# Two MLP products by halves, with seven partial products for eight, weight sums made by accumulating DMAs, and a token-major second product

## The chip, the cores and the metric

The kernel runs on one core of one Trainium2 chip. Times are microseconds of device time; a matmul means one instruction of TensorE. The kernel moves its data between DRAM and the core's on-chip memory (SBUF) by DMA, and TensorE writes its sums into PSUM, of which eight banks are in use.

## What is computed

One layer of a hybrid decoder on 512 tokens of width 2048: a norm, three token mixers, gates, a merge, an output projection with a residual, then a norm and an MLP with a residual, then a last norm. The change concerns the end of it, all in float32:

```python
x = x + merged @ w_out[l]
h = rmsnorm(x, norm_mlp[l])
x = x + jnp.square(jax.nn.relu(h @ mlp_w1[l])) @ mlp_w2[l]
return rmsnorm(x, final_norm)
```

`mlp_w1` is 2048 x 8192 and `mlp_w2` 8192 x 2048. With 512 tokens these two products are the largest of the layer.

## The kernel before

**Exact halves.** TensorE gets no plain float32. Each operand is split into a high part (a cast to `float32r`, ScalarE, `hl` L810 and `wtiles` L731) and a low part (operand minus high part, VectorE, `sub` L32). A product of two tiles is then three matmuls that add into the same bank: high x high, high x low, low x high (L748 to L750).

**Weights.** `wtiles` loads a slab of 128 x 1024 (512 KB) by a DMA on SP's queue into `wraw` (three buffers), and splits it into `whi` and `wlo` (three buffers each). In the answers of the trace these are `wrw`, `whw` and `wlw` for both MLP products. `gemm` (from L736) takes a slab's eight weight tiles as the stationary operand and 512 tokens as the moving operand: 24 matmuls a slab.

**The MLP.** Features lie on the partitions and tokens run along the row. After the output projection (16 products `wo`), each `x1[j]` is at once scaled by `norm_mlp` and split into `hh` and `ho`, beside the next product. The 1/rms factor R is not in these operands; it is multiplied in later, at the hidden layer. Eight rounds c follow. Each makes 8 hidden tiles `w1_f` (16 slab tiles deep, two slabs each), applies relu, R and a square on ScalarE and VectorE, splits the result into `ah` and `al`, and then runs 16 products `w2_c_j` of 8 tiles each, whose sums VectorE adds to `x1[j]` (L29). In the last round the products 8 to 15 run in two halves of 256 tokens, so that the final norm of the first half lies beside the second. The output leaves feature-major and is transposed on the host.

**What sets the order.** TensorE's order is the program's. On the other engines a list scheduler places instructions at build time, by priority and by its own estimate of when their inputs come; each engine then executes its list strictly in that order and waits where an input is missing. `high_priority` puts the weight path in front. SP's queue issues all DMAs of the kernel.

**Memory.** `acts` holds 32 tiles of the split activations, `stage` three work tiles, `mlp` the residual and part of the split operands. PSUM has two banks for `gps` tiles and six for `ps` tiles.

## Time and profile before

| | us |
|---|---|
| median of three runs | 3062.14 |
| lowest and highest run | 3059.55, 3068.38 |
| span of the profiled execution | 3059.8 |
| TensorE busy in it | 3001.3 |
| VectorE, ScalarE, GpSimd busy | 1557.3, 989.0, 336.8 |
| each of the three groups of matmuls of the first MLP product (`w`<-`hh`, `ho`; about 1024 each), busy | 398 to 399 |

The profiled execution has no other time than its span; it lies within the three runs. A matmul's own duration is longer than the distance to the next one, since matmuls overlap; for time on TensorE the distance between two starts is what counts. The MLP takes the span from about 1650 us to the end.

### The profile page before, as it was taken

To read this page: it belongs to the slowest core of one execution; us is meant where nothing else is said; L and a number is where in the kernel's file an instruction comes from. 1 tells how busy PE (TensorE), PEld (TensorE's weight loads), DVE (VectorE), ACT (ScalarE), POOL (GpSimd) and SP (SyncE) were. 2 spreads that over 40 slices of the span, in tenths; PEclk is the share of its full clock that TensorE was granted. 3 is DMA by queue.
4 is the path that set the end of the run, shared out by engine and by line. 5 is a ranking of instruction groups with operands and counts; after the bars stand their busy time and mean duration, and the time that the engine had idled before them with its cause. 6 is when DMAs were issued, how large, how long until landed. Compare 5 with 4: busy or idle time off the path is not lost.

```text
span 3059.8 us, 36455 instructions
## 1 busy us (share of the span) xinstructions
PE 3001.3 (98%) x14143; PEld 2468.2 (81%) x14143; DVE 1557.3 (51%) x2350; ACT 989.0 (32%) x1224; POOL 336.8 (11%) x572
## 2 busy tenths in 40 slices
PE   8999988999999999999999999999999999999997
PEld 7888776788877777888888888888888888888887
DVE  7766888855664555555334334333333434333335
ACT  6554121234662233422223222122222212222235
POOL 1001766530000000011110000000000000000003
PEclk9999988999999999999999999999999999999999
DMA  5345333445337163655432333333233323323334
GB/s 181 124 162 185 114 103 98 136 131 166 102 103 190 55 186 97 229 165 170 157 98 94 97 99 96 99 98 97 97 97 97 97 96 97 97 96 97 97 97 151
DMA packets 172638, 370.72 MB, mean 121 GB/s; under 512 B 63377, under 2 KB 74385, under 8 KB 171665
## 3 DMA queue, kind: packets, MB, share of 16 engines
q1 hardware_dynamic: 172464, 368.38, 38.2%
q8 instruction: 112, 1.84, 0.3%
q14 instruction: 62, 0.50, 0.1%
HBM read 318.81 MB, written 44.58 MB: 119 GB/s over the span
## 4 chain that ended last, share of the span: by engine, by line
PE 85%; DVE 6%; POOL 3%; DMA 3%; SPq 1%; issue 1%; ACT 0%; DVEq 0%; ACTq 0%; POOLq 0%
PE w L748 15%; PE w L749 15%; PE w L750 15%; PE gt L748 5%; PE gt L750 5%; PE gt L749 5%; PE z L748 2%; PE z L750 2%; PE z L749 2%; PE wo L750 2%; PE up L748 2%; PE wo L748 2%; PE up L750 2%; PE up L749 2%; PE wo L749 2%
## 5 line engine op out<-in xcount | busy, mean ns | idle before, releaser
L731 ACT CAST whw<-wrw 128x1024 fp32r<-128x1024 f32 x264 | 278.0, 1053 | 885.8 <-PE w L749 872.4
L32 DVE TENSOR_TENSOR wlw<-wrw,whw 128x1024 fp32r<-128x1024 f32 x264 | 324.1, 1227 | 405.2 <-ACT whw L731 405.2
L748 PE MATMUL w<-ah,whw 128*128 128x512 f32 (+1 forms) x1088 | 409.9, 377 | 0.1
L750 PE MATMUL w<-ah,wlw 128*128 128x512 f32 (+1 forms) x1088 | 409.7, 377 | 0.0
L749 PE MATMUL w<-al,whw 128*128 128x512 f32 (+1 forms) x1088 | 409.7, 377 | 0.0
L748 PE MATMUL w<-hh,whw 128*128 128x512 f32 x1024 | 398.7, 389 | 0.0
L750 PE MATMUL w<-hh,wlw 128*128 128x512 f32 x1024 | 398.4, 389 | 0.0
L749 PE MATMUL w<-ho,whw 128*128 128x512 f32 x1024 | 398.4, 389 | 0.0
L748 PE MATMUL gt<-uh,whgt 128*128 128x512 f32 x768 | 310.6, 404 | 2.8 <-DVE gz L26 2.8
L750 PE MATMUL gt<-uh,wlgt 128*128 128x512 f32 x768 | 300.6, 391 | 2.0 <-DVE wlgt L32 2.0
L749 PE MATMUL gt<-ul,whgt 128*128 128x512 f32 x768 | 300.2, 391 | 0.0
L29 DVE TENSOR_TENSOR x<-x,w 128x512 f32<-128x512 f32 (+1 forms) x136 | 89.2, 656 | 388.0 <-PE w L750 388.0
L748 PE MATMUL z<-uh,whin 128*128 128x512 f32 x608 | 243.7, 401 | 11.8 <-DVE zs L26 11.8
L750 PE MATMUL z<-uh,wlin 128*128 128x512 f32 x608 | 241.0, 396 | 8.1 <-DVE wlin L32 8.1
L749 PE MATMUL z<-ul,whin 128*128 128x512 f32 x608 | 240.0, 395 | 0.0
L748 PEld LDWEIGHTS w<-ah,whw 128*128 128x128 f32 x1088 | 204.7, 188 | 37.7 <-issue 0.2
L749 PEld LDWEIGHTS w<-al,whw 128*128 128x128 f32 x1088 | 204.7, 188 | 37.5
L750 PEld LDWEIGHTS w<-ah,wlw 128*128 128x128 f32 x1088 | 204.7, 188 | 37.4
L748 PEld LDWEIGHTS w<-hh,whw 128*128 128x128 f32 x1024 | 192.2, 188 | 40.2 <-issue 0.2
L749 PEld LDWEIGHTS w<-ho,whw 128*128 128x128 f32 x1024 | 192.2, 188 | 40.1 <-issue 0.2
L750 PEld LDWEIGHTS w<-hh,wlw 128*128 128x128 f32 x1024 | 192.2, 188 | 39.9
L29 POOL TENSOR_TENSOR acc<-acc,sq 128x512 f32<-128x512 f32 x29 | 49.7, 1713 | 1521.7 <-ACT sq L830 1490.7
(442 smaller groups left out, 4577.8 us busy)
## 6 DMA issues: line engine op xcount, KB each, us to landing
wrw<-in_w SPq DMA_DIRECT2D x264, 512.0 KB, 3.6
wrgt<-in_w_in SPq DMA_DIRECT2D x96, 512.0 KB, 4.0
wrin<-in_w_in SPq DMA_DIRECT2D x76, 512.0 KB, 3.6
wrup<-in_w_up SPq DMA_DIRECT2D x32, 512.0 KB, 4.0
wrwo<-in_w_out SPq DMA_DIRECT2D x32, 512.0 KB, 3.6
gd<-gz SPq DMA_DIRECT2D x48, 256.0 KB, 2.2
gl<-gd SPq DMA_DIRECT2D x48, 256.0 KB, 3.1
zd<-zs SPq DMA_DIRECT2D x21, 256.0 KB, 2.0
```

The lines of the kernel that those rows point to most:

```text
L29: (eng or self.nc.vector).tensor_tensor(out, a, b, ALU.add)
L32: (eng or self.nc.vector).tensor_tensor(out, a, b, ALU.subtract)
L731: nc.scalar.copy(hi, raw)
L748: nc.tensor.matmul(ps, hi[:, ws], xh, start=first, stop=False)
L749: nc.tensor.matmul(ps, hi[:, ws], xl, start=False, stop=False)
L750: nc.tensor.matmul(ps, lo[:, ws], xh, start=False, stop=last)
```

## The change

Both products are made by halves. A product of two matrices, each cut into four quadrants, takes eight products of quadrants; here it takes seven, of sums of quadrants, and the results are combined by additions (the scheme of Strassen and Winograd). The partial products are numbered 1 to 7. Their operands are, for the weights W: 1 is W11, 5 is W11+W12, 6 is W11+W12+W22, 4 is W11+W12+W22+W21, 3 is W22, 7 is W22+W12, 2 is W21. They run in the order 1, 5, 6, 3, 7, 2, 4.

**Weight sums.** `wsums` holds tile A for 1, 5, 6 and 4, tile B for 3 and 7, and tile C for 2. Three quadrants are loaded plainly on SP's queue. The other four are added onto what A or B holds, in place, by DMAs with `accum_op=ALU.add`, which GpSimd issues. After each load or addition the tile is split into `whi` and `wlo`, which still have three buffers each; A has four, B and C share the three of `wraw`.

**First product.** The tokens are halved (256) and the features are halved. After the output projection, `hsums` forms four sums of two scaled tiles on VectorE and splits all seven operands into `hch` and `hcl` (1792 columns). Three of eight tiles are made during the output projection; five lie in memory that the output projection still uses. The unscaled `x1` is transposed by TensorE (16 groups of four), copied by ScalarE and stored to DRAM as `x1d`, token-major. Then 32 units u follow, each of seven products of 24 matmuls with a moving operand of 256 columns, in three banks `ha`, `hc`, `hb`. Banks are used on: product 6 adds onto product 1 in `ha` after ScalarE has copied it to `pk1`, and so on. VectorE combines the results in `hy`, applies relu and the square, and the 512 KB go to DRAM as `hid`. 1/rms squared is applied only after the second product, by `R2`, one value a token.

**Second product.** It is token-major: the activations are the stationary operand, the weights the moving one, 512 columns. Each round c reads four `hid` tiles back; GpSimd forms their sums in `aG`, ScalarE and VectorE split them into `ah` and `al` (six buffers each). For each half n of the output, two weight chains (`ph` 0 and 1, called a and b) run beside each other: a product is 24 matmuls, 12 with a's weights and 12 with b's. For n = 0 the first two products of a stand ahead of those of b. VectorE adds each bank, scaled by `R2`, to the residual `xT`. The last norm works on rows of tokens, and the output needs no transposition.

```diff
+    ORDER = (1, 5, 6, 3, 7, 2, 4)
+    PLACE = {1: 0, 4: 1, 2: 2, 5: 3, 6: 4, 7: 5, 3: 6}
+    BANK = {1: "a", 6: "a", 7: "a", 4: "a", 5: "c", 3: "c", 2: "b"}
+    def sums(self, G, hi, lo, eng=None):
+        a21, a11, a22, a12, s1, s2, s3, s4 = (G[:, q] for q in range(8))
+        self.sub(s1, a21, a22, eng)
+        self.sub(s2, s1, a11, eng)
+        self.sub(s3, a11, a21, eng)
+        self.add(s4, s2, a12, eng)
+        self.hl(G[:, 1:].rearrange("p q t -> p (q t)"), hi, lo)
+    def wsums(self, name, B, pool, order=None):
+        nc = self.nc
+        at = {}
+        def load(c, q):
+            p = pool if c == "A" else None
+            at[c] = (p or self.wp).tile([P, 1024], F32, name=f"w{c}{name}", tag="wA" if p else "wraw", bufs=self.wA if p else self.wraw)
+            nc.sync.dma_start(at[c], B[q])
+            return at[c]
+        def acc(c, q):
+            nc.gpsimd.dma_start(at[c], B[q], accum_op=ALU.add)
+            return at[c]
+        how = {1: lambda: load("A", "11"), 5: lambda: acc("A", "12"), 6: lambda: acc("A", "22"),
+               4: lambda: acc("A", "21"), 3: lambda: load("B", "22"), 7: lambda: acc("B", "12"),
+               2: lambda: load("C", "21")}
+        for i in order or self.ORDER:
+            with self.tc.high_priority(self.wprio):
+                x = how[i]()
+                hi = self.wp.tile([P, 1024], F32R, name=f"wh{name}_{i}", tag="whi", bufs=self.whl)
+                lo = self.wp.tile([P, 1024], F32R, name=f"wl{name}_{i}", tag="wlo", bufs=self.whl)
+                nc.scalar.copy(hi, x)
+                self.sub(lo, x, hi)
+            yield i, hi, lo
+    def w1_mm(self, ps, i, w, hc, ks):
+        for k in ks:
+            ws = slice(k * P, k * P + P)
+            g = slice(256 * self.PLACE[i], 256 * self.PLACE[i] + 256)
+            for q, (a, b) in enumerate(((0, 0), (0, 1), (1, 0))):
+                self.nc.tensor.matmul(ps, w[a][:, ws], hc[k][b][:, g], start=i in (1, 5, 2) and k == 0 and q == 0,
+                                      stop=k == 7 and q == 2, skip_group_check=True)
+    def w1_out(self, u, i, bank, keep, pool, hid):
+        nc = self.nc
+        with self.tc.high_priority(2 * self.wprio):
+            if i in (1, 5, 6):
+                keep[i] = pool.tile([P, 256], F32, name=f"pk{i}_{u}", tag=f"pk{i}", bufs=2)
+                nc.scalar.copy(keep[i], bank[self.BANK[i]])
+            if i == 1:
+                keep["y"] = pool.tile([P, 4, 256], F32, name=f"hy{u}", tag="hy", bufs=2)
+            y = keep["y"]
+            if i == 7:
+                self.sub(y[:, 2], keep[5], bank["a"])
+            elif i == 2:
+                self.add(y[:, 1], bank["b"], keep[1])
+            elif i == 3:
+                self.sub(y[:, 3], bank["c"], keep[6])
+            elif i == 4:
+                nc.scalar.copy(y[:, 0], bank["a"])
+                f = y.rearrange("p q t -> p (q t)")
+                self.stt(f, f, 0.0, f, ALU.max, ALU.mult)
+                nc.sync.dma_start(hid, f)
...
-                        nc.scalar.activation(hi, x1[j], AF.Copy, scale=col("norm_mlp", j))
-                        self.stt(lo, x1[j], col("norm_mlp", j), hi, ALU.mult, ALU.subtract)
+                    if j in (8, 9, 10):
+                        hsums(j - 8)
+                trunk.close()
+                for k in range(3, 8):
+                    hsums(k)
...
+                    for u in range(1, 32):
+                        bank, keep = banks(u), {}
+                        for i, *w in self.wsums(f"u{u}", w1_quadrants(u), mp):
+                            self.w1_mm(bank[self.BANK[i]], i, w, hc, range(8))
+                            self.w1_out(u, i, bank, keep, mp, hid[u])
...
+                    def hidden(u):
+                        with tc.high_priority(2 * self.wprio):
+                            G = mp.tile([P, 8, 256], F32, name=f"aG{u}", tag="aG", bufs=2)
+                            nc.sync.dma_start(G[:, 0:4].rearrange("p q t -> p (q t)"), hid[u])
+                            r = [mp.tile([P, 1792], F32R, name=f"a{q}{u}", tag=f"a{q}", bufs=6) for q in "hl"]
+                            self.sums(G, *r, nc.gpsimd)
+                        return r
+                    def mm2(ps, i, w, aa, ph, t):
+                        for p in range(2):
+                            x = aa[2 * ph + p]
+                            g = slice(256 * self.PLACE[i] + P * t, 256 * self.PLACE[i] + P * t + P)
+                            ws = slice(T * p, T * p + T)
+                            for q, (a, b) in enumerate(((0, 0), (1, 0), (0, 1))):
+                                nc.tensor.matmul(ps, x[a][:, g], w[b][:, ws], start=i in (1, 5, 2) and ph + p + q == 0,
+                                                 stop=ph + p + q == 4, skip_group_check=True)
...
+                            for (i, *w), (_, *w1) in zip(*gens):
+                                for t in range(2):
+                                    ps = bank[self.BANK[i]][t]
+                                    mm2(ps, i, w, aa, 0, t)
+                                    mm2(ps, i, w1, aa, 1, t)
+                                    out2(i, n, ps, t)
```

The scheduler places the rest. On ScalarE, in the middle of the first product, before: casts of slabs (`whw1_f`) and, for each hidden tile, a relu and a cast.

```order
L731 CAST whw1_21_0_15937<-wrw1_21_0_15935 128x1024
L1156 ACTIVATE a19_15857<-w1_19_15796 128x512
L810 CAST ah19_15861<-a19_15857 128x512
L731 CAST whw1_21_8_15967<-wrw1_21_8_15965 128x1024
L731 CAST whw1_22_0_16006<-wrw1_22_0_16004 128x1024
L1156 ACTIVATE a20_15926<-w1_20_15865 128x512
L810 CAST ah20_15930<-a20_15926 128x512
```

The same engine now, unit 17: `whu17_i` is the high part of operand i, `pk1`, `pk5` and `pk6` are copies of banks after products 1, 5 and 6.

```order
L806 CAST whu17_1_17441<-wAu17_17439 128x1024
L836 COPY hy16_17249<-ha16_17214 128x256
L806 CAST whu17_5_17473<-wAu17_17439 128x1024
L825 COPY pk1_17_17469<-ha17_17436 128x256
L825 COPY pk5_17_17501<-hc17_17437 128x256
L806 CAST whu17_6_17504<-wAu17_17439 128x1024
L806 CAST whu17_3_17536<-wBu17_17534 128x1024
L825 COPY pk6_17_17532<-ha17_17436 128x256
L806 CAST whu17_7_17566<-wBu17_17534 128x1024
L806 CAST whu17_2_17597<-wCu17_17595 128x1024
L806 CAST whu17_4_17627<-wAu17_17439 128x1024
```

Before, the casts stood ahead of the work on finished hidden tiles; now the cast of operand 6 stands behind the copy of the bank of product 5. It stands so in 30 of the units 1 to 31.

VectorE at the same place, before: the slabs' subtractions between the work on the hidden tiles.

```order
L32 TENSOR_TENSOR wlw1_21_0_15938<-wrw1_21_0_15935,whw1_21_0_15937 128x1024
L26 TENSOR_TENSOR a19_15857<-a19_15857,R_81 128x512
L26 TENSOR_TENSOR a19_15857<-a19_15857 128x512
L32 TENSOR_TENSOR al19_15862<-a19_15857,ah19_15861 128x512
L32 TENSOR_TENSOR wlw1_21_8_15968<-wrw1_21_8_15965,whw1_21_8_15967 128x1024
```

VectorE now, unit 17: `wlu17_i` is the low part of operand i, `hy17` the combination of the unit's results.

```order
L33 TENSOR_TENSOR wlu17_5_17474<-wAu17_17439,whu17_5_17473 128x1024
L33 TENSOR_TENSOR wlu17_6_17505<-wAu17_17439,whu17_6_17504 128x1024
L33 TENSOR_TENSOR wlu17_3_17537<-wBu17_17534,whu17_3_17536 128x1024
L33 TENSOR_TENSOR hy17_17471<-hc17_17437,pk6_17_17532 128x256
L33 TENSOR_TENSOR wlu17_7_17567<-wBu17_17534,whu17_7_17566 128x1024
L33 TENSOR_TENSOR wlu17_2_17598<-wCu17_17595,whu17_2_17597 128x1024
L33 TENSOR_TENSOR wlu17_4_17628<-wAu17_17439,whu17_4_17627 128x1024
```

In 21 of the units 1 to 31 the subtraction for operand 7 stands behind the combination that reads product 3's bank, as here. On GpSimd, where the first product had nothing but sums of squares, four accumulating DMAs a unit now stand in the order 5, 6, 4, 7, each behind the splits that read its tile.

ScalarE in the second product, at the beginning of round c = 1 (`whv100` are a's weights for n = 0, `whv101` b's, `ah6` and `ah7` the round's third and fourth activation tiles, `ah8` and `ah9` the next round's first):

```order
L806 CAST whv100_1_21400<-wAv100_21398 128x1024
L887 CAST ah6_21116<-aG6_21114 128x1792
L887 CAST ah7_21126<-aG7_21124 128x1792
L806 CAST whv100_5_21417<-wAv100_21398 128x1024
L806 CAST whv101_1_21435<-wAv101_21433 128x1024
L887 CAST ah8_21664<-aG8_21662 128x1792
L806 CAST whv101_5_21454<-wAv101_21433 128x1024
L806 CAST whv100_6_21473<-wAv100_21398 128x1024
L887 CAST ah9_21674<-aG9_21672 128x1792
L806 CAST whv101_6_21478<-wAv101_21433 128x1024
```

Before, ScalarE had only the casts of weights in the second product, apart from the last round; now the casts of activations stand between them.

## Rows read from the trace of the kernel before

**Rows 1.** The page, busy us by engine, and the granted clock in 40 slices.

```profile
PE 3001.3 (98%) x14143; PEld 2468.2 (81%) x14143; DVE 1557.3 (51%) x2350; ACT 989.0 (32%) x1224; POOL 336.8 (11%) x572
PEclk9999988999999999999999999999999999999999
```

**Rows 2.** Stages: us, busy time of each engine, clock, DMA share, GB/s.

```profile
core 0: us, PE busy (x) PEld busy (x) DVE busy (x) ACT busy (x) POOL busy (x), PEclk, DMA share, GB/s
1600.00:1700.00 100.00, 100.00 (x441) 82.44 (x440) 40.49 (x44) 33.01 (x40) 8.74 (x5) 1.00 0.29 97
1700.00:2000.00 300.00, 300.00 (x1325) 248.42 (x1324) 112.90 (x123) 71.33 (x79) 0.00 (x0) 1.00 0.31 98
```

**Rows 3.** Timeline of TensorE, 512 columns: start, duration, instruction; 36 steps apart.

```profile
2984.21 0.39 PE L748 MATMUL w<-ah,whw 128*128 128x512 f32 x1
...
2992.37 0.39 PE L748 MATMUL w<-ah,whw 128*128 128x512 f32 x1
```

**Rows 4.** The same timeline, 256 columns; 48 steps apart.

```profile
3009.80 0.28 PE L748 MATMUL w<-ah,whw 128*128 128x256 f32 x1
...
3015.57 0.28 PE L748 MATMUL w<-ah,whw 128*128 128x256 f32 x1
```

**Rows 5.** Waits of SP's queue: who waited, for whom, us, times, longest.

```profile
SPq L728 <- DVE wlw L32: 1271.6, 253, 9.1
```

**Rows 6.** Groups by line and shape: busy us, mean ns, idle before.

```profile
L731 ACT CAST whw<-wrw 128x1024 fp32r<-128x1024 f32 x264 | 278.0, 1053 | 885.8 <-PE w L749 872.4 <-PE wo L749 8.8 <-issue 4.6
L32 DVE TENSOR_TENSOR wlw<-wrw,whw 128x1024 fp32r<-128x1024 f32 x264 | 324.1, 1227 | 405.2 <-ACT whw L731 405.2
L285 ACT COPY s5es<-s5e 128x256 f32<-128x256 f32 x12 | 4.5, 373 | 15.4 <-PE s5e L276 15.4
L29 DVE TENSOR_TENSOR x<-x,w 128x256 f32<-128x256 f32 x16 | 6.7, 418 | 5.2 <-PE w L750 5.2
L260 ACT COPY s5ET<-s5ETp 128x512 f32<-128x512 f32 x12 | 7.0, 584 | 20.1 <-PE s5ETp L259 20.0
L1137 ACT ACTIVATE hh<-x,pcol 128x512 fp32r<-128x512 f32 x16 | 11.3, 718 | 0.0
L26 POOL TENSOR_TENSOR x<-x,rt 128x256 f32<-128x256 f32 x20 | 19.6, 1017 | 33.6 <-DVE rt L42 33.6
```

**Rows 7.** DMA issues: KB each, median us from issue to landing.

```profile
wrw<-in_w SPq DMA_DIRECT2D x264, 512.0 KB, 3.6
dBKT<-BKT SPq DMA_DIRECT2D x5, 512.0 KB, 2.9
BKTl<-dBKT SPq DMA_DIRECT2D x5, 512.0 KB, 6.8
```

**Rows 8.** Stages at the end, columns as in rows 2.

```profile
3042.00:3044.00 2.00, 1.60 (x12) 1.19 (x10) 0.70 (x2) 0.46 (x2) 2.00 (x3) 1.00 0.51 181
3044.00:3046.00 2.00, 0.70 (x2) 0.30 (x2) 0.42 (x1) 1.25 (x4) 0.94 (x2) 1.00 0.42 153
3046.00:3060.00 14.00, 0.00 (x0) 0.00 (x0) 7.49 (x15) 1.45 (x2) 3.55 (x4) 0.59 0.49 165
```

**Rows 9.** A wait of TensorE in the timeline, and the stages behind it.

```profile
328.19 1.12 PE L259 MATMUL s5ETp<-cst,s5E 128*128 128x128 f32 x4 [3.07 <-POOL s5E L32]
326.00:328.00 2.00, 0.00 (x0) 0.00 (x0) 2.00 (x3) 0.00 (x0) 1.92 (x2) 1.00 0.19 76
328.00:330.00 2.00, 1.81 (x8) 1.29 (x9) 2.00 (x7) 0.59 (x1) 0.14 (x1) 0.55 0.02 4
330.00:332.00 2.00, 2.00 (x9) 1.27 (x8) 2.00 (x7) 0.57 (x1) 0.00 (x0) 0.60 0.10 39
332.00:334.00 2.00, 2.00 (x11) 1.62 (x10) 1.97 (x7) 1.05 (x1) 0.22 (x1) 1.00 0.61 223
```

More of the change, by code (lines that the diff above doesn't have):

```diff
@@ L1 @@
+import contextlib
 import math
@@ new lines, in banks @@
+                def banks(u):
+                    return {q: self.ps(f"h{q}{u}")[:, 0:256] for q in "acb"}
+                gen = self.wsums("u0", w1_quadrants(0), None, (1, 5, 2, 6, 3, 7, 4))
+                bank, keep = banks(0), {}
+                three = [next(gen) for _ in range(3)]
+                for i, *w in three:
+                    self.w1_mm(bank[self.BANK[i]], i, w, hc, range(3))
+                for jb in (0, 2, 1, 3):
+                    for t in range(4):
+                        pt = self.gps(f"xt{jb}{t}")
+                        for q in range(4):
+                            nc.tensor.transpose(pt[:, q * P:q * P + P], x1[4 * jb + q][:, t * P:t * P + P], self.ident)
+                        st = fp.tile([P, T], F32, name=f"xs{jb}{t}", tag="xs", bufs=2)
+                        nc.scalar.copy(st, pt)
+                        nc.sync.dma_start(x1d[t][:, T * jb:T * jb + T], st)
@@ new lines, in main @@
+                pm = self.gps("pms")
+                for t in range(4):
+                    nc.tensor.matmul(pm[:, 2 * t:2 * t + 2], acc[:, t * P:t * P + P], self.onesD[:, 0:2], start=True, stop=True)
+                self.ts(R2, pm[:, 0:8:2], 1e-6, ALU.add)
+                nc.vector.reciprocal(R2, R2)
+                front.close()
+                with mixpool("w1", "right") as mp:
+                    for i, *w in three:
+                        self.w1_mm(bank[self.BANK[i]], i, w, hc, range(3, 8))
+                        self.w1_out(0, i, bank, keep, mp, hid[0])
+                    for i, *w in gen:
+                        self.w1_mm(bank[self.BANK[i]], i, w, hc, range(8))
+                        self.w1_out(0, i, bank, keep, mp, hid[0])
+                    for u in range(1, 32):
+                        bank, keep = banks(u), {}
+                        for i, *w in self.wsums(f"u{u}", w1_quadrants(u), mp):
+                            self.w1_mm(bank[self.BANK[i]], i, w, hc, range(8))
+                            self.w1_out(u, i, bank, keep, mp, hid[u])
@@ L1269, in pack @@
     r["w1"] = slabs(i["mlp_w1"][0], 16)
[L1270 removed]
+    w2 = i["mlp_w2"][0].reshape(8, 2, 2, 2, 128, 2, 2, 512)
+    r["w2"] = np.ascontiguousarray(w2.transpose(0, 6, 1, 3, 5, 4, 2, 7)).reshape(8, 2, 2, 2, 2, 128, 1024)
+    r["final_row"] = np.ascontiguousarray(np.broadcast_to(i["final_norm"][None], (128, 2048)))
     r["glu"] = slabs(i["s5_glu_w"][0], 6)
```

198 lines of the change are left out of this document (104 added, 94 removed).

## Prediction

> **What bounds the kernel now.** I read the page's busy shares first: TensorE is busy 3001.3 of 3059.8 us and its clock row shows full speed nearly everywhere [rows 1]. The table by stages says the same of the MLP: TensorE 300 of 300 us, VectorE 112.90, ScalarE 71.33, the DMA engines at a share of 0.31 for 98 GB/s [rows 2]. Even the hand-over from the output projection to the MLP, between 1600 and 1700, holds no gap [rows 2]. So time in the MLP is matmuls times their step. The timeline of TensorE gives the steps: 36 matmuls of 512 columns in 8.16 us, 0.2267 each [rows 3], and 48 of 256 columns in 5.77 us, 0.1202 each [rows 4]: half the columns cost 53% of the step. The weights are never late: every load of a w slab waits first for the subtraction that frees its buffer, 253 waits, 1271.6 us [rows 5].
>
> **TensorE's own work.** First product, before: 64 x 16 x 3 = 3072 matmuls of 512 columns, 696.4 us, or 21.76 for each of what are now 32 units. After: a unit is 7 products x 8 slabs x 3 matmuls of 256 columns, 168 x 0.1202 = 20.19 us; in all 5376 and 646.2. Second product, before: 2880 of 512 and 384 of 256 columns, 652.9 + 46.2 = 699.1 us. After: 16 passes x 7 x 24 = 2688 of 512, 609.4 us. If TensorE never waits, the gain is 50.2 + 89.7 = 140 us. Seven for eight is 12.5%, but the narrow moving operand takes nearly half of that back in the first product.
>
> **The first product's weights.** Before, each slab had its own load, far ahead. Now four of a unit's seven operands come by adding in place onto the operand before: 1, 5, 6 and 4 in one tile A, 3 and 7 in B. An accumulating DMA may start only when the cast and the subtraction have read the tile, and the next cast only when it has landed. There are three high and three low buffers, so the split of a product cannot begin before TensorE has finished the product three places earlier; the operand of product 1 is therefore split only at the end of the previous unit's 7. From there runs one chain: split 1, add, split 5, add, split 6, subtraction of 3, add (into B), split 7, and the rest of product 7's matmuls, which free the buffer again. A split is a cast of 1.053 and a subtraction of 1.227, 2.28 us [rows 6]; the third matmul needs the low part, so 22 of 24 matmuls, 2.64 us, follow it. With L for one accumulation and 0.4 us for eight hand-overs, the period is 4 x 2.28 + 1.23 + 2.64 + 0.4 + 3L = 13.4 + 3L us. TensorE's 20.19 us hide this only up to L = 2.3.
>
> L has no row. Below: it is a 512 KB load and more, so at least the plain load's 3.6 us [rows 7]; less is excluded. Above: a 512 KB store (2.9) and a load in company (6.8), 9.7 [rows 7]. It is nearest to the plain load plus one more pass of 512 KB, since it reads the old tile as well. At 98 GB/s for a share of 0.31 the engines pass 316 GB/s, so a pass is 1.7 us, and L = 5.3. The add into B (operand 7) is issued 1.23 us behind the fourth add into A (operand 4) on GpSimd's queue and shares the engines with it; I put half of a two-pass transfer, 1.7 us, on it. The period is 13.4 + 15.9 + 1.7 = 31.0 us against 21.76: **+296 us over 32 units.** Each further us of L costs 96.
>
> The Trainium skill bears on L. "DMA: Bandwidth & Descriptors" (Anatomy of one DMA) fits about 2.0 us + bytes/436e3 for a DMA that GpSimd issues, and "Collectives: The Full Stack" (why ReduceScatter is half of AllGather) says that an add needs two source reads. By these an estimate is 2.0 + 2 x 1.2 = 4.4 us, a period of 28.3 and +209, and some 3300 us in all; no run here shows it yet.
>
> **The queues' order** sets a floor under this, whatever L is. In 30 of the 31 later units ScalarE's cast of operand 6 stands behind the copy of product 5's bank, which waits for TensorE. So after product 5 come the drain (0.16), a copy (0.373), a cast and a subtraction, less two matmuls: 2.6 us in which TensorE does nothing. Behind the waiting cast stand casts 3 and 7. In 21 units VectorE's subtraction for 7 stands behind the combination of product 3's bank (0.418) [rows 6]: 1.6 us. Floor: 20.19 + 2.6 + 1.1 = 23.9 us, +68 us over the stage. At L = 5.3 the chain is longer and hides it.
>
> The bank copies (four of 0.373 us a unit), the combinations and the 512 KB store of `hid` lie beside other work: VectorE needs some 11.5 us of a unit, ScalarE 9. The three plain loads of a unit are issued a unit ahead on SP; nothing there is late.
>
> **The second product's weights.** The same three buffers serve two chains, a and b. A pair of half products is 24 matmuls, 5.44 us. Chain b may split 1 when the pair before is at three quarters, and must have 6 ready 6 + 2 matmuls into its pair: 1.36 + 10.88 + 1.81 = 14.05 us for 3 x 2.28 + 2L = 17.4, short by 3.4; operand 7 of b is short by 2 x 2.28 + L - 8.61 = 1.3. So 4.7 us in a pass with n = 1. In a pass with n = 0 the first four half products come singly, and the splits of two activation tiles (1792 columns, by scaling 1.84 and 2.15 us) stand among them on ScalarE and VectorE. Following the same rule I get 2.2 for operand 5 of a, 3.4 and 3.6 for 5 and 6 of b, 1.4 for 7: 10.6. Eight times 15.3 is 122 us against the 89.7 won: **+33 us.** With L = 3.6 the waits are some 7 us per two passes, and the stage is 32 us faster; each us of L costs 50 to 56.
>
> **The hand-overs.** Before they cost nothing [rows 2]. Into the first product: tiles 3 to 7 of `hc` lie in memory that the output projection reads to its end. Per tile two scaled copies (1.44), four sums (1.7), a cast (1.84) and a subtraction (2.15) run in turn through one `hG`, 7.1 us; the 16 copies of the transposes (0.584 each [rows 6]) fit between. Four of these and 4.0 for the first, less 3.2 us of early matmuls: **+29 us** (20 to 40). Into the second: `aG` lies in `hc`'s memory, so the load (3.6), six GpSimd sums at 1.02 [rows 6], a cast and a subtraction come after the last matmul; the third and fourth tile wait for `aG` to come free. The fourth is ready at about 27.5 us, with 5.4 us of matmuls before it: **+22 us** (12 to 35). The end stays: today 15 us from the last matmul to the end [rows 8]; after, the scaling of the last tiles, four table loads and a store give about the same.
>
> **Sum.** 296 + 33 + 29 + 22 = +380 on the profiled span of 3059.8, which is 2.3 below the median of the runs: 3440 in it, 3442 in runs. I say 3440.
>
> **Rivals.** *Short accumulation.* If L is 3.6 to 4.3 the chain is 24.2 to 26.3, hardly over the floor: +78 to +145; the second product -32 to +10; hand-overs +45: 3150 to 3270. For it: the load's 3.6 already holds all fixed time. Against: a second pass and an issue by GpSimd, neither of which the plain load has.
>
> *The DMA engines become the bound.* In a pass of the second product 6 loads and 8 adds of two passes are 11.5 MB; at 316 GB/s that is 36.5 us against 38.1 of TensorE. If an add takes a third pass, it is 50 us, the second product takes 800 us, and in the first L grows past 7.3, period 37 and more: 3670 to 3850. For it: the tightness. Against: 316 GB/s is no proven limit.
>
> *A falling clock.* One wait of 3.07 us of TensorE was followed by 0.55 and 0.60 of granted clock, near 1.2 GHz, for about 4 us [rows 9]. Here product 6 waits 3 to 4 us in each unit. Product 6 at half rate is 2.9 us later, but 7 waits for its add anyway; I count at most 1.2 us a unit, 38 us, inside the range.
>
> *Faster after all: everything is hidden.* With L under 2.3 the period falls below 20.19; if besides the copies and casts of the floor overlap, the stages give 140 back and the hand-overs cost 45 to 51: 2970. It decides at L = 2.3. Against it stand the plain load's 3.6 [rows 7] and the queues' order; with the order alone the same L gives 3060 to 3110.
>
> **How the numbers follow.** Forecast (L from 4.3 to 7, 3270 to 3670): 0.61. Short accumulation: 0.18. Engines as the bound: 0.16. Hidden and faster: 0.03. Hidden but held by the order to no change: 0.02. The range leaves out the slow end of the bound's case and the hidden ones: 3180 to 3720. Measurement tells apart about 0.3%. Faster 0.03, same 0.02, slower 0.95.
>
> **What would show it.** In the profile after: matmuls of the first product at a step near 0.12 us but with idle time of TensorE before products 5, 6 and 7, released by ScalarE's casts and those by DMA; the time from issue to landing of the adds near 5.3 us; 32 equal periods near 31 us. Periods near 24 say the order alone binds; near 20 that all is hidden and I am wrong. The second product should take 720 to 750 us with waits at operands 5 and 6 of b. A DMA share near 1 would speak for the engines, a granted clock under 0.9 over the first product for the third rival. Wrong most easily: L, which has no row, and whether the add into B is late behind the one into A.

## The result

The changed kernel takes 3652.43 us (median; 3064.17 for the kernel before), a ratio of 1.1905 with an interval of 1.1882 to 1.1928: a fifth slower. One of the four runs took 3768.1 us at a granted clock of 0.80 (0.92 to 0.93 in the others); it is left out of the ratio, but not of the median. The forecast was 3440, with a range of 3180 to 3720. The sign, the mechanism and the main price were as forecast; the loss is half as large again (+588 us for +380).

The page of the changed kernel, busy us by engine and the granted clock in 40 slices; before, TensorE was at 98% [rows 1]:

```profile
span 3650.7 us, 41666 instructions
PE 3138.7 (86%) x15933; PEld 2612.1 (72%) x15933; DVE 1897.2 (52%) x2607; ACT 1202.9 (33%) x1451; POOL 658.7 (18%) x929
PEclk9999989999999999997888888888887999999998
```

Its issues of DMAs (KB each, and the median time from issue to landing):

```profile
wAu<-in_w POOLq DMA_DIRECT2D x96, 512.0 KB, 5.5
wAv<-in_w POOLq DMA_DIRECT2D x96, 512.0 KB, 5.5
...
wCu<-in_w SPq DMA_DIRECT2D x32, 512.0 KB, 4.0
wBu<-in_w POOLq DMA_DIRECT2D x32, 512.0 KB, 7.0
```

`wAu`, `wBu`, `wCu` are the tiles A, B, C of the first product, `wAv` those of the second. L, the number without a row, is there now: an addition of 512 KB lands 5.5 us after its issue in A and 7.0 in B; 5.3 and 5.3 + 1.7 were put in. The Trainium skill's "DMA: Bandwidth & Descriptors" (Anatomy of one DMA), with two reads for an addition, gave an estimate of 4.4; the trace says 5.5, and the trace decides.

Two stages of the changed kernel (us, busy time of the engines, clock, DMA share, GB/s): the first product with its head, and the second with its hand-over and the end.

```profile
core 0: us, PE busy (x) PEld busy (x) DVE busy (x) ACT busy (x) POOL busy (x), PEclk, DMA share, GB/s
1651.00:2770.00 1119.00, 831.35 (x5453) 787.00 (x5451) 360.13 (x374) 289.43 (x380) 111.44 (x128) 0.84 0.53 124
2770.00:3651.00 881.00, 701.97 (x2690) 520.33 (x2688) 529.66 (x510) 306.05 (x305) 242.60 (x256) 0.92 0.70 162
```

The MLP's first matmul stands at 1645.7 us before and at 1651.8 now; these 6 us arise ahead of the output projection, where the instructions are the same, and the forecast has no term for them. The first product was forecast at 696 + 296 + 29 = 1021 us and took 1119; the rest at 699 + 33 + 22 and 17 from the last matmul to the end, 771, and took 881. So both stages are about 100 us over. Two groups give the periods: the last operation on a unit's hidden values (32 of them) and the scaled addition of product 2's banks (two a pass, 16 passes); min, median and max in ns, then the first and the last start.

```profile
L43 DVE SCALAR_TENSOR_TENSOR hy<-hy x32: 1218/1226/1226, 1712.7 to 2770.6; 128x1024 f32<-128x1024 f32 x32
L43 DVE SCALAR_TENSOR_TENSOR xT<-ob,R,xT x32: 744/748/753, 2849.5 to 3612.3; 128x512 f32<-128x512 f32 x32
```

A unit takes (2770.6 - 1712.7) / 31 = 34.13 us; 31.0 was forecast. A pass takes (3612.3 - 2849.5 - 3.4) / 15 = 50.6 us by this group (3.4 is the distance of a pass's two). That is too little: the last pass runs product 2 two places earlier, so that its distance is 33.9 us; the other 14 average 51.8. Below, a pass is counted from its first matmul to the next pass's, as the mean of rounds 1 to 6: 57.0 us for n = 0 and 47.1 for n = 1, where 38.1 + 10.6 = 48.7 and 38.1 + 4.7 = 42.8 were forecast.

### The profile page after: what moved, and what is told of

The parts are those of the page before. It is cut to its first block, busy times and chain, and to the rows that moved or that the text cites. A ratio compares the mean times of both kernels' runs of the same rounds, so it can differ in the third digit from the quotient of the medians.

```text
span 3650.7 us, 41666 instructions
## 1 busy us (share of the span) xinstructions
PE 3138.7 (86%) x15933; PEld 2612.1 (72%) x15933; DVE 1897.2 (52%) x2607; ACT 1202.9 (33%) x1451; POOL 658.7 (18%) x929
## 5 line engine op out<-in xcount | busy, mean ns | idle before, releaser
L816 PE MATMUL ha<-hch,whu 128*128 128x256 f32 x1024 | 347.1, 339 | 193.1 <-ACT whu L806 180.0
L816 PEld LDWEIGHTS ha<-hch,whu 128*128 128x128 f32 x1024 | 245.4, 240 | 206.3 <-ACT whu L806 192.2
L816 PE MATMUL ha<-hch,wlu 128*128 128x256 f32 x1024 | 347.6, 339 | 36.6 <-DVE wlu L33 36.6
L816 PE MATMUL ha<-hcl,whu 128*128 128x256 f32 x1024 | 338.8, 331 | 0.0
L816 PEld LDWEIGHTS ha<-hch,wlu 128*128 128x128 f32 x1024 | 246.4, 241 | 51.4 <-DVE wlu L33 51.4
L1298 PE MATMUL oa<-whv,ah 128*128 128x512 f32 x512 | 214.3, 418 | 54.9 <-ACT whv L806 33.0
L816 PEld LDWEIGHTS ha<-hcl,whu 128*128 128x128 f32 x1024 | 246.7, 241 | 0.2 <-DVE hcl L33 0.2
L1298 PE MATMUL oa<-wlv,ah 128*128 128x512 f32 x512 | 214.0, 418 | 23.8 <-DVE wlv L33 23.6
L33 DVE TENSOR_TENSOR wlv<-wAv,whv 128x1024 fp32r<-128x1024 f32 x128 | 159.2, 1254 | 137.9 <-ACT whv L806 137.8
L1298 PE MATMUL oa<-whv,al 128*128 128x512 f32 x512 | 209.4, 409 | 5.1 <-DVE al L33 5.1
```

Of the source, the lines that this page charges most:

```text
L33: (eng or self.nc.vector).tensor_tensor(out, a, b, ALU.subtract)
L816: self.nc.tensor.matmul(ps, w[a][:, ws], hc[k][b][:, g], start=i in (1, 5, 2) and k == 0 and q == 0, stop=k == 7 and q == 2, skip_group_ch ...
L1298: nc.tensor.matmul(ps, x[a][:, g], w[b][:, ws], start=i in (1, 5, 2) and ph + p + q == 0, stop=ph + p + q == 4, skip_group_check=True)
```

## One unit of the first product

ScalarE in one unit of the changed kernel (start, duration, instruction; in brackets how long it waited, and for what):

```profile
2206.14 1.05 ACT L806 CAST whu<-wBu 128x1024 fp32r<-128x1024 f32 x1 [3.58 <-DMA wBu<-in_w]
...
2213.39 1.05 ACT L806 CAST whu<-wAu 128x1024 fp32r<-128x1024 f32 x1 [4.30 <-PE ha L816]
...
2221.62 1.05 ACT L806 CAST whu<-wAu 128x1024 fp32r<-128x1024 f32 x1 [1.38 <-DMA wAu<-in_w]
...
2229.72 1.05 ACT L806 CAST whu<-wAu 128x1024 fp32r<-128x1024 f32 x1 [2.44 <-DMA wAu<-in_w]
...
2240.59 1.05 ACT L806 CAST whu<-wBu 128x1024 fp32r<-128x1024 f32 x1 [3.85 <-DMA wBu<-in_w]
```

These are the casts of 7, 1, 5, 6 and the next 7: the chain of the prediction, and every one waits for a DMA, or (1) for product 7's matmuls, which free the buffer. The distances are 7.25, 8.23, 8.10 and 10.87 us, 34.45 in all; forecast were 4.9, 7.6, 7.6 and 10.5, and 0.4 for hand-overs. GpSimd issues the additions between them:

```profile
2215.98 0.86 POOL L796 DMA_DIRECT2D wAu<-in_w  x1 [15.89 <-DVE wlu L33]
2224.22 0.86 POOL L796 DMA_DIRECT2D wAu<-in_w  x1 [7.38 <-DVE wlu L33]
2232.32 0.86 POOL L796 DMA_DIRECT2D wAu<-in_w  x1 [7.24 <-DVE wlu L33]
2233.46 0.86 POOL L796 DMA_DIRECT2D wBu<-in_w  x1 [0.27 <-DVE wlu L33]
```

From the issue of the first to the cast that reads it are 5.64 us. Each issue stands 0.29 us behind the end of the subtraction that it waits for (2214.46 + 1.23 for the first). So a link of the chain is some 0.6 us longer than was put in. As means of 30 units the four steps are 6.48, 8.42, 8.27 and 11.10 us. The fourth issue is 1.14 us behind the third and its tile is read 7.1 us later: the order A, B on GpSimd's queue, as forecast. The largest difference is in the step from 7 to 1. TensorE in it, 20 steps apart:

```profile
2208.88 0.41 PE L816 MATMUL ha<-hch,whu 128*128 128x256 f32 x1
...
2213.15 0.41 PE L816 MATMUL ha<-hch,wlu 128*128 128x256 f32 x1
```

0.2135 us a step for the 0.1202 of [rows 4]: behind the wait the granted clock is 0.50 (1.2 GHz), and product 7's matmuls, which the chain passes through, take 2 us longer in this unit. Whether that is a cause or only shows the wait is the first question below.

## Experiments

The period of a unit is worked out from the same group as above.

### Is the low clock on the chain?

```diff
                         for i, *w in self.wsums(f"u{u}", w1_quadrants(u), mp):
+                            fill({6: 28, 7: 24}.get(i, 0))
...
```

`fill(n)` makes n matmuls of 256 columns into a bank that nobody reads.

> Extra matmuls into a spare bank stand ahead of product 6 (28 of them, 3.4 us) and of product 7 (24, 2.9 us) in every unit of the first product, where TensorE waits today; nothing reads them. In the trace of the changed kernel a unit takes 34.15 us, and product 7's matmuls run at a granted clock of 0.50 for some 5 us behind the wait. Theory A (the low clock lies on the chain of splits and additions): with TensorE busy in the waits the clock stays up, product 7's 22 matmuls take 2.6 us for 4.9, the period falls by about 2.3 to 31.9 us, the whole to about 3580. Theory B (the price as the prediction had it, at most 1.2 us a unit and most of that hidden): 3615 to 3650. Theory C (the extra matmuls get in the way, or the clock falls for another reason than the wait): 3650 or more.

Measured: 3697 us, ratio 1.2069 (1.2049 to 1.2089). A unit takes 35.46 us, longer than without the extra matmuls. That is theory C's time, but the test was not clean: behind the remaining waits the clock still fell. So a second run with more of them:

```diff
+                            fill({5: 20, 6: 36, 7: 44}.get(i, 0))
```

> As the first run with extra matmuls, but enough of them that TensorE should hardly wait at all: 20 ahead of product 5, 36 ahead of 6, 44 ahead of 7 in each unit (12.0 us; with the 20.2 of the products 32.2 us). In the first such run waits of 1.5 to 3 us remained ahead of products 5 and 7, the clock still fell to 0.50 behind them, additions in A took 6.3 us for 5.5 and the period was 35.5 us. Theory A (the low clock behind product 7's wait lengthens the chain by 2.3 us): granted clock near 1.00, period 32.2 to 32.8 us, whole 3585 to 3610. Theory B (the clock isn't on the chain, only the additions' landing is): period 34 to 36, 3650 to 3700.

Measured: 3668 us, ratio 1.1969 (1.1945 to 1.1993). The group of the units and a stage of this run (columns as in the stages above):

```profile
L43 DVE SCALAR_TENSOR_TENSOR hy<-hy x32: 1218/1226/1226, 1713.4 to 2776.7; 128x1024 f32<-128x1024 f32 x32
```

```profile
2000.00:2200.00 200.00, 189.54 (x1551) 185.84 (x1550) 61.92 (x64) 47.03 (x63) 19.01 (x22) 1.00 0.56 124
```

The clock is 0.99 to 1.00 throughout, and a unit takes 34.30 us all the same. Theory B's time. As means of 30 units, the step from the cast of 7 to that of 1 fell from 6.48 to 5.46 us, but the three with additions grew from 8.42, 8.27 and 11.10 to 9.14, 8.57 and 11.29. So the low clock does lengthen the one step, by some 1.0 us, and keeping the clock up in this way doesn't shorten the unit: the additions took as much back. Why they then take longer was not settled; in the unit looked at the addition for 5 starts 3 us behind the issue of the last of the next unit's three plain loads, which land some 4 to 6 us after their issue; in the changed kernel it starts 5 us behind it.

### What in L is the addition?

```diff
-            nc.gpsimd.dma_start(at[c], B[q], accum_op=ALU.add)
+            nc.gpsimd.dma_start(at[c], B[q])
```

> The four additions a unit (and eight a pass of the second product) become plain loads into the same tiles, by the same queue and with the same waits; the sums are left out, so the partial products are made of single quadrants. Theory A (the addition makes the transfer longer: 5.5 us in A and 7.0 in B where plain loads of 512 KB take 3.6 to 4.1): landing falls to about 4.0, the period of a unit by 4 to 6 us, the second product by some 60 to 80 us, the whole to 3380 to 3470. Theory B (the length comes from GpSimd's issue, 0.86 us, and the queue, and adding costs nothing): landing stays near 5.5 and the time near 3650.

Measured: 3397.69 us, ratio 1.1093 (1.1071 to 1.1115); a unit takes 29.05 us. Landing and a stage of this run, and last the same stage of the changed kernel:

```profile
wAu<-in_w POOLq DMA_DIRECT2D x96, 512.0 KB, 4.1
wAv<-in_w POOLq DMA_DIRECT2D x96, 512.0 KB, 4.0
...
wBu<-in_w POOLq DMA_DIRECT2D x32, 512.0 KB, 5.5
```

```profile
2200.00:2400.00 200.00, 163.10 (x1164) 155.50 (x1163) 74.13 (x77) 58.61 (x77) 14.84 (x28) 0.91 0.44 148
```

```profile
2200.00:2400.00 200.00, 150.68 (x998) 143.12 (x997) 62.19 (x64) 48.74 (x64) 19.12 (x23) 0.85 0.54 125
```

Theory A. Of 5.5 us, 4.1 are a plain load by the same queue and 1.4 are the addition. The engines' time says the same: 0.54 x 34.13 = 18.4 us a unit with additions, 0.44 x 29.05 = 12.8 without. Eight plain transfers then take 1.6 us each, and an addition 1.4 more. The Trainium skill's "Collectives: The Full Stack" (why ReduceScatter is half of AllGather) puts the price of an add into its second source read; the trace agrees, with 1.9 times a plain load's time of the engines.

### Is the chain the whole loss?

```diff
         def acc(c, q):
-            nc.gpsimd.dma_start(at[c], B[q], accum_op=ALU.add)
-            return at[c]
+            return load(c, q)
```

> Each operand is loaded plainly into a tile of its own by SP's queue, a unit ahead; the sums are left out. The chain of split, addition, split is gone, the order of the queues stays. Theory A (the chain is nearly all of the loss, under it lies the floor of the queues' order at 23.9 us a unit): first product -10 us a unit, -325; second product -80 to -130; 3190 to 3250. Theory B (the order costs nothing once the chain is gone): 20.2 us a unit, -445, in all 3070 to 3130. Theory C (the DMA engines or the splits of the activations hold it): above 3400.

Measured: 3040.3 us, ratio 0.9926 (0.9907 to 0.9946). The groups and a stage:

```profile
L43 DVE SCALAR_TENSOR_TENSOR hy<-hy x32: 1217/1219/1224, 1695.7 to 2313.2; 128x1024 f32<-128x1024 f32 x32
L43 DVE SCALAR_TENSOR_TENSOR xT<-ob,R,xT x32: 743/749/751, 2382.1 to 2998.7; 128x512 f32<-128x512 f32 x32
```

```profile
2000.00:2200.00 200.00, 200.00 (x1685) 200.00 (x1684) 110.09 (x111) 84.32 (x111) 0.00 (x0) 1.00 0.67 212
```

Theory B, and below its range: 19.92 us a unit, with no gap of TensorE in the first product; a pass takes 45.2 us for n = 0 and 39.1 for n = 1. The chain and what it brings with it is 612 us. Two things follow. The floor of 23.9 us that the prediction read from the order isn't there: without the chain the build puts the cast of 6 ahead of the copy of 5's bank in all 31 units, so the order was a result of the late additions. And even with the sums left out, the kernel is only 0.7% faster than before: of the 140 us that TensorE saves, the head (30 us), the hand-over (13 us to the second product's first matmul) and the waits of the second product (692 us for 609 of matmuls) eat all but some 22.

### Place in the order or number of buffers?

Five high and five low buffers in the first product, order unchanged:

```diff
-                hi = self.wp.tile([P, 1024], F32R, name=f"wh{name}_{i}", tag="whi", bufs=self.whl)
+                if name[0] == "u" and pool is not None and n % 5 > 2:
+                    hi = pool.tile([P, 1024], F32R, name=f"wh{name}_{i}", tag="whx", bufs=2)
...
```

> The changed kernel with five high and five low weight buffers in the first product for three (two of each in the stage's own memory; tile A has three buffers for four), order 1, 5, 6, 3, 7, 2, 4 as it was. Theory A (the chain of split and addition 1, 5, 6, 3, 7 binds, and the buffers only add the wait of split 1 for product 7's matmuls): the chain runs 8.2 + 8.1 + 10.9 us and some 2 us of casts from 7 to the next 1, 29.3 us a unit for 34.15, -155 us, 3495. Theory B (the buffers are the cause, and with five of them the additions are hidden): 20 to 24 us a unit, 3200 to 3320. Theory C (buffers don't matter): 34, 3650.

Measured: 3511.77 us, ratio 1.1459 (1.1436 to 1.1482). A unit takes 29.72 us: theory A to 0.4 us. The chain binds with five buffers as well. In part two changes cancel in the sum: in the 18 units whose additions keep their order on GpSimd's list, the time from the issue of the addition for 7 to that of the next one for 5 falls from 16.3 to 10.0 us; but the link behind it grows from 8.55 to 10.38, as the addition for 5 lands after 7.2 us for 5.8.

Then the order, in the second product alone:

```diff
-                            order = (1, 5, 6, 2, 3, 7, 4) if last else self.ORDER
+                            order = (1, 5, 6, 2, 3, 7, 4) if last else (1, 2, 5, 3, 6, 7, 4)
```

> Second product alone: the partial products run in the order 1, 2, 5, 3, 6, 7, 4 (the last pass as it was), so that another product stands between 1 and 5 and between 5 and 6, which use one tile after another addition. In the trace of the changed kernel a pass takes 47.0 us for n = 1 and 56.6 for n = 0, for 38.1 of matmuls. Theory A (the chain of additions is the wait in both): n = 1 falls to 39 to 41, n = 0 by 5 to 9 us, -100 us in all, 3550. Theory B (in n = 0 it is the activations: their sums on GpSimd and their splits): only n = 1 gains, -50, 3600. Theory C (order doesn't matter): 3650.

Measured: 3524.35 us, ratio 1.151 (1.1479 to 1.154); a pass takes 48.3 us for 57.0 with n = 0 and 39.1 for 47.1 with n = 1. That is 128 us for one line. Theory A, a little more than it gave.

In both products (the first needs two more places for results):

```diff
-    ORDER = (1, 5, 6, 3, 7, 2, 4)
+    ORDER = (1, 2, 5, 3, 6, 7, 4)
+    BANK1 = {1: "a", 6: "a", 4: "a", 2: "b", 7: "b", 5: "c", 3: "d"}
...
```

> Both products in the order 1, 2, 5, 3, 6, 7, 4. In the first product that needs products 3 and 7 in banks of their own (a fourth bank, and 2's again) and two more small subtractions and one more copy a unit; everything else, the accumulating DMAs too, stays. Between two splits of one tile stand two products, 5.8 us, and the split may begin two products before its own matmuls. Theory A (the loss is where the additions stand in the order, not their length: split to split 8.2 us against 11.5 us from split 1 to the matmuls of 5): TensorE no longer waits, 20.0 to 21.5 us a unit for 34.15, first product -400 to -450; with the second product's gain (3524) 3075 to 3125. Theory B (each link is still late by 8.2 less 5.8): 27 us a unit, 3300. Theory C (the transfers themselves bind): above 3400.

Measured: 3303.48 us, ratio 1.0778 (1.0762 to 1.0794), a unit 27.09 us: theory B's numbers, but not by its reason. ScalarE in one unit (casts of the last unit's 4 with this unit's 1, then 5, 6, and 4 with the next 1):

```profile
2103.86 1.99 ACT L807 CAST whu<-wAu 128x1024 fp32r<-128x1024 f32 x2 [4.67 <-DMA wAu<-in_w]
...
2113.55 1.05 ACT L807 CAST whu<-wAu 128x1024 fp32r<-128x1024 f32 x1 [6.21 <-DMA wAu<-in_w]
...
2121.82 1.04 ACT L807 CAST whu<-wAu 128x1024 fp32r<-128x1024 f32 x1 [6.00 <-DMA wAu<-in_w]
...
2130.01 1.99 ACT L807 CAST whu<-wAu 128x1024 fp32r<-128x1024 f32 x2 [4.59 <-DMA wAu<-in_w]
```

Split to split is 8.2 us, three links a unit, and the next unit's 1 stands right behind this unit's 4 in the list: one chain after the other, 26.2 us here. Space between the links gains no more while the chains of successive units stand in line. So two units were interleaved:

```diff
-                    for u in range(1, 32):
+                    for us in [(u, u + 1) for u in range(1, 31, 2)] + [(31,)]:
...
+                        for both in zip(*gens):
+                            for (u, bank, keep), (i, *w) in zip(st, both):
...
```

> First product: two units u and v run interleaved, product by product, in the order 1, 2, 5, 3, 6, 7, 4 (1 of u, 1 of v, 2 of u, ...), with the old banks; accumulating DMAs as before; second product in the new order. In the run with both orders a unit took 27.1 us, since one unit's additions in tile A (1, 5, 6, 4) follow the last unit's on ScalarE's list: three links of 8.2 us and the next cast. Theory A (that chain is the period): two chains run side by side, 26.6 us of chain against 40.4 us of matmuls for two units, TensorE waits no more, 20.2 to 20.8 us a unit and 3070 to 3100 in all. Theory B (the DMA engines: in the changed kernel a unit keeps them at a share of 0.54 for 34.2 us, 18.5 us; at 20.2 that is 0.91): landing grows to 7 us and more, 21.5 to 24 us a unit, 3120 to 3200.

Measured: 3096.04 us, ratio 1.0096 (1.0081 to 1.0111). Its group of units, a stage and two rows on landing:

```profile
L43 DVE SCALAR_TENSOR_TENSOR hy<-hy x32: 1216/1218/1226, 1704.2 to 2330.8; 128x1024 f32<-128x1024 f32 x32
```

```profile
2000.00:2200.00 200.00, 200.00 (x1685) 200.00 (x1684) 109.21 (x111) 84.25 (x111) 34.60 (x40) 1.00 0.90 211
```

```profile
wAu<-in_w POOLq DMA_DIRECT2D x96, 512.0 KB, 5.8
wBu<-in_w POOLq DMA_DIRECT2D x32, 512.0 KB, 5.8
```

Theory A: 20.21 us a unit with every accumulating DMA in place. 556 of the 588 us are gone by the order of the work alone. Theory B falls: at a share of 0.90 the additions land only 0.3 us later in A (5.8 us for 5.5), and in B they land earlier (5.8 for 7.0).

### Additions on VectorE instead

```diff
         def acc(c, q):
-            nc.gpsimd.dma_start(at[c], B[q], accum_op=ALU.add)
+            if vec:
+                old = at[c]
+                self.add(load(c, q), at[c], old)
...
```

> First product in the old order, but each quadrant is loaded plainly, by SP's queue, into a tile of its own, and VectorE adds it to the tile before (four additions of 128x1024 a unit); no accumulating DMA there. Second product: accumulating DMAs in the new order. Theory A (only the additions' place in the chain mattered; on VectorE they can be made ahead of the splits): 19.9 to 20.5 us a unit, as in the run with tiles of their own and no sums (3040); the second product some 20 us behind that run; 3055 to 3075. Theory B (VectorE's queue: seven subtractions, four additions and five combinations are some 16 us of a 20 us unit, and each waits in line): 22 us a unit and more, 3120 and more.

Measured: 3157.2 us, ratio 1.0303 (1.0286 to 1.032); a unit takes 22.34 us. Theory B. VectorE is busy 133.34 of 200 us in the stage from 1800, but TensorE's longest waits between 1720 and 2300 are for its combinations (`hy`), which stand in line behind additions and subtractions:

```profile
PE ha L820 <- DVE hy L33: 25.7, 16, 2.7
PE hc L820 <- DVE wlu L33: 10.5, 21, 1.2
```

### The second product's activations and the hand-over

Sums of activations on VectorE for GpSimd, on top of both orders:

```diff
-                            self.sums(G, *r, nc.gpsimd)
+                            self.sums(G, *r)
```

> As the run with both orders, and the activations' sums of the second product on VectorE for GpSimd. In the run with the second product's new order a pass with n = 0 still takes about 46.8 us (n = 1: 40.1), and while GpSimd adds there VectorE's subtractions take 1.8 to 3.3 us for 1.23 and GpSimd's own sums 1.6 to 2.4 for 1.03. Theory A (the two engines slow each other down, and GpSimd's additions by DMA stand behind its sums): n = 0 falls to 41 to 43, -30 to -45 us against the run with both orders. Theory B (VectorE, at 7 of 10 busy, becomes the bound with 16 more sums a round, 7 us): no gain or up to 30 us slower.

Measured: 3300.45 us, ratio 1.0775 (1.0747 to 1.0803): no change against 3303.48, as theory B had it. But what theory A started from does go away: the two engines no longer slow each other, as the low part's subtraction shows in the run before and in this one (min, median and max in ns):

```profile
L33 DVE TENSOR_TENSOR al<-aG,ah x32: 2012/2026/2603, 2555.3 to 3193.3; 128x1792 fp32r<-128x1792 f32 x32
```

```profile
L33 DVE TENSOR_TENSOR al<-aG,ah x32: 2014/2020/2027, 2551.6 to 3191.5; 128x1792 fp32r<-128x1792 f32 x32
```

Nor do the sums hold the additions any more: the second addition of a pass with n = 0 is issued 7.0 us after the pass's first matmul, for 11.2 in the run before. Only, it lands after 8.3 us for 5.7 (means of rounds 1 to 6). One of them, and the cast that reads it:

```profile
2843.94 0.86 POOL L797 DMA_DIRECT2D wAv<-in_w  x1 [8.76 <-DVE wlv L33]
...
2851.96 1.04 ACT L807 CAST whv<-wAv 128x1024 fp32r<-128x1024 f32 x1 [7.88 <-DMA wAv<-in_w]
```

So TensorE's wait ahead of product 5 falls only from 6.8 to 5.5 us a pass, and the one ahead of 3, for a weight's low part that stands behind an activation's on VectorE, grows from 0.2 to 3.6. A pass with n = 0 takes 48.9 us for 47.8. Then smaller transfers at the hand-over, on top of VectorE's additions:

```diff
+                    def xload(n):
+                        for t in (2, 3, 0, 1):
+                            v, w = (x.rearrange("p (h c) -> p h c", h=2)[:, :, T * n:T * n + T] for x in (xT[t], x1d[t]))
+                            nc.sync.dma_start(v, w)
...
+                    xload(0)
```

> As the run with VectorE's additions, and at the hand-over to the second product: only the half of the residual that the first pass needs is loaded there (2 MB for 4), the other half behind the fourth activation tile, the row for the last norm in round 6, and the sums of the first four activation tiles on VectorE. In the runs so far the DMA engines are at a share of 1.0 for 32 us there, and the loads of the third and fourth activation tile land 16 to 20 us after their issue. Theory A (the transfers in the way are the hand-over's cost): 10 to 18 us less, 3040 to 3060, faster than the kernel before by up to 0.8%. Theory B (the splits of the four tiles set it, or the half loads come late for the second pass): no change, 3055 to 3075.

Measured: 3149.87 us, ratio 1.0273 (1.0257 to 1.0288), 7 us under the run without. The two profiled executions lie 14.6 us apart, and 5 of these are in the first product. A hint for theory A, and by the runs less than it gave. Last, all that helped, with the sums of activations shared:

```diff
-                            self.sums(G, *r, nc.gpsimd)
+                            self.sums(G, *r, None if u < 4 or u % 4 > 1 else nc.gpsimd)
...
```

> The run with interleaved units (3096), with the smaller transfers at the hand-over from the run before it (only half of the residual there, the last norm's row later), and in the second product the activations' sums shared: VectorE those of the first four tiles and of the third and fourth of every round, GpSimd the others. In the run with interleaved units TensorE waits 4.7 to 5.1 us ahead of product 5 in every pass with n = 0, and on GpSimd's list additions by DMA stand behind sums of activations, which take 2.3 to 4.1 us a tile there. Theory A (those sums hold the additions): 2 to 4 us a round and 6 us at the hand-over, 3060 to 3080. Theory B (in n = 0 it is the DMA engines, at a share of 0.85 to 0.95 there, as the run with all sums on VectorE suggests, which gained nothing): only the hand-over's 6 us, 3085 to 3095. Theory C (VectorE is late with the sums as well): 3096 and more.

Measured: 3086.13 us, ratio 1.0068 (1.0053 to 1.0084): theory B's time, and still slower than the kernel before. From the last unit's relu to the first addition of product 2's bank it takes 44.7 us for 55.7 in the run with interleaved units, and a pass with n = 0 takes 47.2 us for 48.1. Against this, the MLP's first matmul stands at 1655.0 us for 1644.3, though none of the edits touches what lies ahead of the output projection; why was not tried. In the profiles of all the kernels here this point lies anywhere between 1644.3 and 1655.0, so a few us between two whole times say nothing of the MLP; the stages have to be compared. No version beat the kernel before with the sums in it.

## Why the prediction was right, and what it missed

**TensorE's own work** was right: 20.21 us a unit where nothing waits (20.19 forecast). So was the head: 1119 us less 32 periods is 27, for 29.

**The first product's chain** was right in its links, its order and its bound: taking the chain out, spacing it, running two side by side and giving it buffers gave the periods that the links make. L was right to 0.2 us, and so was the delay of the addition into B (1.5 us by the landing, 7.0 for the 5.5 of plain loads at the same place, where 1.7 were put in). Mis-sized was the period, 34.1 for 31.0. By the means of 30 units the three steps with additions take 27.8 us for 25.7, for the issue behind the subtraction and a slightly longer landing, and the step through product 7 takes 6.5 for 4.9; the 0.4 us for hand-overs go off this. The prediction allowed a falling clock up to 1.2 us a unit, and its sign of that, a granted clock under 0.9 over the first product, is there (0.84). It looked for the cost at product 6; on the chain it is product 7 that runs slowly. With TensorE kept busy this step is some 1.0 us shorter, about the size that was counted; but the additions then took longer, and whether the unit would be shorter at a full clock without the extra matmuls isn't shown.

**The floor of the queues' order** was a misreading: an order that a scheduler made for late additions is no bound on a kernel without them. It cost nothing in the sum, since the chain was longer.

**The second product** was mis-sized most in its steady passes, 57.0 us for 48.7 with n = 0 and 47.1 for 42.8 with n = 1: 85 us over the 14 passes between the first and the last. The term is the sum of TensorE's waits. With n = 0 it waits 9.2 us ahead of operand 5 of b, for 3.4 in the prediction; 2.9, 3.5 and 2.6 ahead of 5 of a, 6 and 7, for 2.2, 3.6 and 1.4. With n = 1 it waits 2.3 us ahead of 5, which had no wait in the prediction, and 3.9 and 2.3 ahead of 6 and 7 for 3.4 and 1.3. In the changed kernel, around the start of a round, GpSimd issues two of the additions between sums of activations, and the casts that need them come 7.6 to 8.9 us after the issues, not 5.3:

```profile
3225.03 0.86 POOL L796 DMA_DIRECT2D wAv<-in_w  x1
...
3225.64 1.03 POOL L30 TENSOR_TENSOR aG<-aG 128x256 f32<-128x256 f32 x1
...
3226.33 1.18 POOL L796 DMA_DIRECT2D wAv<-in_w  x1
...
3233.89 1.99 ACT L806 CAST whv<-wAv 128x1024 fp32r<-128x1024 f32 x2 [5.50 <-DMA wAv<-in_w]
...
3234.99 0.80 PE L1298 MATMUL oc<-whv,ah 128*128 128x512 f32 x1 [7.43 <-ACT whv L806]
```

TensorE waits 7.43 us there. The prediction priced every addition alone, at one L; at a round's start they run in company with four loads of activations. The share of the chain in this is shown: the new order took 128 us away. What is left with n = 0 is not the additions alone. In the run with tiles of its own, which has none, such a pass still takes 45.2 us for 38.1 of matmuls, at a DMA share of 0.65 in the one from 2513.5. There TensorE waits for the low part of b's operand 6, and its cast stands behind the cast of an activation tile, which waits for GpSimd's sums:

```profile
2524.78 1.70 ACT L886 CAST ah<-aG 128x1792 fp32r<-128x1792 f32 x1 [4.09 <-POOL aG L30]
2526.38 1.04 ACT L805 CAST whv<-wAv 128x1024 fp32r<-128x1024 f32 x1
...
2530.57 0.51 PE L1297 MATMUL oa<-wlv,ah 128*128 128x512 f32 x1 [2.37 <-DVE wlv L33]
```

So the activations' place in the lists is one part. A later landing is another (8.3 us in the run with the sums on VectorE), most likely from the transfers beside it, which was not shown by itself. How the waits divide between the two was not taken apart.

**The hand-over** to the second product was mis-sized too: the prediction followed the activations' splits and left out what stands on the queue with them. The DMA engines are full there:

```profile
2775.00:2783.00 8.00, 0.00 (x0) 0.00 (x0) 1.63 (x1) 2.62 (x2) 5.74 (x7) 0.50 1.02 401
2783.00:2791.00 8.00, 4.22 (x7) 2.23 (x8) 4.05 (x2) 1.80 (x2) 3.50 (x3) 0.50 1.02 393
```

4 MB of the residual, 1 MB of the norm's row and 2 MB of weights lie ahead of the third activation tile on SP's queue. From the first product's last matmul to the end of the first pass it takes 88 us, 17 more than forecast, and the last pass is 8 us over; they were not taken apart further, but half the residual and the sums' move took 11 us out of the hand-over (55.2 to 44.2 us, and 55.7 to 44.7).

**The rivals.** A short accumulation (3.6 to 4.3) is excluded: that is what a plain load takes by the same queue, 4.1. By the time alone the engines as the bound are not excluded, since 3652 lies only 18 us below that rival's range. The profile excludes them for the first product: the share is 0.53 there, and 0.90 cost nothing. They do bind at the hand-over, at a share of 1.02. The clock is judged above.

## What to carry to other kernels

An accumulation in place makes each sum wait for the readers of the one before it. Price such a chain as a ring (split, issue, landing, split) over the whole period and ask where the next period's first link stands in each engine's list; spreading the links gave the first half here (34.1 to 27.1 us a unit), and two chains side by side the rest (20.2). And before sizing a saving of matmuls, price what it brings with it: here a head, a hand-over and the waits for the split activations took all but some 22 of the 140 us even with the chain gone. A mean over passes hides which pass waits; count each kind by itself.

## What the runs showed of the hardware

- An accumulating DMA of 512 KB costs the DMA engines 1.9 times a plain load and lands 1.4 us later (5.5 for 4.1 us, same queue).
- At a DMA share of 0.90 these additions still land in 5.8 us; at the hand-over, at 1.0, the third activation tile of the run with the activations' sums on VectorE was asked for at 2553.61 and first read at 2573.99.
- A step of 256 columns is 0.2135 us at the granted clock of 0.50 and 0.1202 at 1.00.
- VectorE and GpSimd slow each other. The subtraction of 1792 columns takes 2.03 us as a median, and up to 4.84 beside GpSimd's sums; with those sums on VectorE none takes over 2.03. The Trainium skill's "SBUF — State Buffer" (Who interferes with whom) says that a VectorE instruction with two inputs in SBUF contends with a GpSimd instruction that reads it; the rows agree:

```profile
L33 DVE TENSOR_TENSOR al<-aG,ah x32: 2015/2026/4839, 2783.1 to 3531.3; 128x1792 fp32r<-128x1792 f32 x32
L30 POOL TENSOR_TENSOR aG<-aG x32: 715/1602/2612, 2780.7 to 3458.0; 128x256 f32<-128x256 f32 x32
```

These two are of the changed kernel.
